# S5 input products from 32-row pieces of split tiles, and the angle sum issued one chunk ahead

## The chip, the cores and the metric

The kernel runs on one core of a Trainium2 chip. The core has a matrix engine (TensorE: PE for its matmuls, PEld for its weight loads), a vector engine (VectorE, DVE), a scalar engine (ScalarE, ACT), a general engine (GpSimd, POOL), and a queue that issues transfers (SyncE, SP). Each engine works through its own queue in the order in which the program puts its instructions there, and an instruction that waits holds back all that stand behind it.

The metric is the device time in microseconds (us); smaller is better. Beside the median of several runs there is one profiled execution, from which all rows of the profile come.

## The reference, cut to what matters

One decoder block works on 256 tokens of 2048 features in float32: a norm, a wide projection `w_in`, two token mixers (S5 and HGRN2), a gated merge, an output projection, and a gated feed-forward network with a short convolution. The change lies in the S5 mixer. Its 1024 input channels `u` form 64 groups of 16, and each group has 64 complex states:

```python
bu_re = einsum('blgc,gpc->blgp', u, b_re)          # input products
bu_im = einsum('blgc,gpc->blgp', u, b_im)
bb_re = coef_re * bu_re - coef_im * bu_im          # hold coefficients
bb_im = coef_re * bu_im + coef_im * bu_re
s     = associative_scan(abar * s_prev + bb)       # along the 256 tokens
y     = einsum(s_re, c_re) - einsum(s_im, c_im) + d * u
```

The kernel folds the coefficients into the input matrices, and turns the complex recurrence into a real one by rotating inputs and states with tables of sines and cosines of the angle per step.

## The kernel before, in words

**The weight stream.** All large products run over tiles of 128x1024 weights. For each tile SP loads `wr`, ScalarE rounds it to `wh` (line 256), VectorE computes the rest `wl = wr - wh`, and TensorE multiplies high and low parts in three products. `wh` and `wl` have three buffers each, so ScalarE and VectorE can be two tiles ahead. `w_in` has 144 such tiles; in the profile one takes TensorE about 2.7 us.

**The side work.** S5 is a generator, `side_s5`, which the loop over the weight tiles resumes after each tile while a meter of estimated VectorE time is not above the one of TensorE (`_dve_cost`, `_pe_cost`; at most two pauses per tile). The tile scheduler then fixes each engine's order. VectorE operations all show line 106, because a helper records them, and so do TensorE's; they are told apart by their tiles.

**One S5 chunk.** There are eight chunks `ct`, each of 128 input channels, that is four pieces `qq` of 32 channels.

- `tables(ct)` makes the rotation tables: GpSimd adds base angles into the tile `w` (line 734, 128x1024), ScalarE rounds it (line 737, which waits for GpSimd), VectorE reduces it, and ScalarE takes sine and cosine (lines 741 to 743).
- `b_place` and `b_trans` write the chunk's input matrix into `zmat`, transpose it on TensorE (`ax<-cf,zmat`), and split matrix and inputs into high and low parts `bc` and `uc` (ScalarE line 260, then VectorE).
- For each piece, 24 GpSimd copies per chunk (line 754, 32x256) then stack three blocks of 32 rows: high, high and low parts of the matrix into `stB`, and high, low and high parts of the inputs into `stU`. Rows 96 to 127 are zero. One matmul over 128 rows so gives the full product of a piece.
- `b_proj(ct, pair)` issues the four matmuls `bu<-u,u` of two pieces into the PSUM tile `bu` (a single buffer of two banks).
- VectorE multiplies `bu` by the tables, combines, runs the scans, and rotates back; `output` multiplies the states by the output matrices (`ax<-u,u`, on 32 columns each).

The products for the next half chunk are issued before the running half is finished, and a chunk's `b_trans` stands in the first half of the chunk before it. `tables(ct+1)` stands in the second half of chunk `ct`, behind the copies for chunk `ct+1` in GpSimd's queue.

Of the kernel before, what the change touches and what calls it, by code (L numbers as in the profile page):

```python
# [17 lines left out]
P = 128  # L18
# [12 lines left out]
# columns of the constant array  # L31
# [5 lines left out]
def _constants():  # L37
# [12 lines left out]
    # within blocks of 32: per level, the columns in second halves of blocks of 2L; then the diagonal  # L50
# [6 lines left out]
# 1/(2 pi) in parts of twelve bits  # L57
# [18 lines left out]
def _dve_cost(name, args, kw):  # L76
    """Estimated microseconds, for the order in which side work is emitted."""
    out = kw.get("out", args[0] if args else None)
    rate = {"tensor_copy": 0.52, "tensor_scalar": 0.52, "reciprocal": 6.3}.get(name, 1.04)
    n = _free(kw["in_"]) if name == "tensor_reduce" else _free(out)  # L80
    return 0.065 + 1.12e-3 * rate * n


def _pe_cost(name, args, kw):
    if name == "transpose":
        return 0.107
    n, m = _free(args[2]), _free(args[1])
    if args[2].dtype == F32R:
        return 0.109 * max(n, 256) / 256 + (0.1 if n < 256 else 0.0)
    if m == 32:  # L90
        return 0.02 + 0.00042 * n
    return 0.213 * max(n, m) / 128


class Metered:
    """An engine that adds up what its instructions are estimated to take."""
# [14 lines left out]
def kernel(  # L111
# [55 lines left out]
    class Chunks:  # L167
        """[128, n, 256] kept in units of four."""
# [102 lines left out]
    def fm_job(wap, c0, nkc, xs, epi, need=None, extra_load=None, wide=False):  # L271
        """psum[n, t] for 256 columns from c0 on; xs(kc) gives the moving pair, or with wide the high part and
        both side by side: the products of the weights' high part then come in two sums to be added up."""
# [30 lines left out]
    def tm_job(wap, c0, width, nkc, kper, xs, epi, need=None, extra_load=None, apart=False):  # L304
        """psum[t, n] for the columns from c0 on; xs(kc) gives the stationary pair."""
# [4 lines left out]
        for g in range(ng):  # L310
            def mm(st, g=g):
# [10 lines left out]
                # all of a row's products together in a last round of several tiles, else the low parts last  # L322
# [22 lines left out]
    def rstd_of(dst, ssum, n, scale, bias=None):  # L345
        """dst = 1/sqrt(ssum*scale + eps) for [128, n]; a Newton step after the square root."""
# [11 lines left out]
    def broadcast_rows(dst, r):  # L358
        """dst[p, j*128 + t] = r[t, j] on every partition."""
# [18 lines left out]
    def warm_up(n, rhs):  # L378
        # matmuls that nothing reads keep the tensor engine's clock up until the first products
# [3 lines left out]
    def table_up():  # L383
        # the square root's table comes in before x does
# [8 lines left out]
    def x_chunk(g, between=None):  # L393
        """Four chunks of x*g, transposed and in two parts; the rows' norms come in after the products."""
# [19 lines left out]
    def behind_x():  # L414
        """What is emitted here is queued behind the last chunk of x."""
# [29 lines left out]
    def normed(ps):  # L445
        """The products of a feature-major job with the rows' norms."""
# [101 lines left out]
    def exp_parts(new, xin):  # L548
        """expm1 of the reduced argument and the power of two, with exp(x) = (1 + e) * s."""
# [20 lines left out]
    def side_s5():  # L570
        # the matrices, long before they are needed
# [6 lines left out]
        # parameters on columns  # L578
# [13 lines left out]
        # lower bound of the forget gate: softmax over two logits, first entry  # L592
# [30 lines left out]
        # angle per step in turns: multiples of 2^-12 and the rest  # L623
# [25 lines left out]
        # coefficients of the zero-order hold  # L649
# [24 lines left out]
        # base angles of the rotation tables  # L674
# [12 lines left out]
        # input matrices with the coefficients in them  # L687
# [14 lines left out]
        # output matrices, transposed  # L702
# [20 lines left out]
        zero = unit()  # L723
        G.memset(zero[96:128, :], 0.0)
        # rows in three blocks of 32: the high and low parts whose products make up one full product
        stB, stU = ([unit(F32R) for _ in range(2)] for _ in range(2))
        for t_ in stB + stU:
            G.tensor_copy(t_[96:128, :], zero[96:128, :])

        def tables(ct):  # L730
            w, r = unit(), unit()
# [4 lines left out]
            yield  # L736
# [16 lines left out]
        def move(dst, src):  # L753
            G.tensor_scalar(out=dst, in0=src.bitcast(F32), scalar1=1.0, scalar2=0.0, op0=ALU.mult, op1=ALU.add)  # L754

        def b_trans(ct):
# [3 lines left out]
            bc, uc = tmp(F32R), tmp(F32R)  # L760
            split_pair(bc[:, 0:T], bc[:, T:2 * T], ax[:, 0:2 * P])
            split_pair(uc[:, 0:T], uc[:, T:2 * T], u_t.at(ct))
            sB, sU = v3(stB[ct % 2], 4), v3(stU[ct % 2], 4)
            for qq in range(4):
                for j in range(3):
                    rows_from, rows_to = slice(32 * qq, 32 * qq + 32), slice(32 * j, 32 * j + 32)
                    hb, hu = (0, 0, 1)[j], (0, 1, 0)[j]
                    move(sB[rows_to, qq, :], bc[rows_from, hb * T:(hb + 1) * T])
                    move(sU[rows_to, qq, :], uc[rows_from, hu * T:(hu + 1) * T])

        def b_proj(ct, pair):
            bu = psb.tile([P, 2, 512], F32, tag="bu", name=f"bu{uid[0]}")
            uid[0] += 1
            sB, sU = v3(stB[ct % 2], 4), v3(stU[ct % 2], 4)
            for a in range(2):
                qq = 2 * pair + a
                for i in range(2):
                    PE.matmul(bu[:, a, i * T:(i + 1) * T], sB[:, qq, i * P:(i + 1) * P], sU[:, qq, :],
                              start=True, stop=True)
            return bu  # L780

        def output(ct, rot):
            """Issues the products of the states of chunk ct and returns what follows them."""
# [23 lines left out]

        tab = yield from tables(0)
# [8 lines left out]
        for ct in range(8):  # L817
            rot = []
            sn, cs = tab
            for pair in range(2):  # L820
# [7 lines left out]
                # the next products, long before they are read  # L828
# [37 lines left out]
    def side_hgrn():  # L866
# [9 lines left out]
        # scores: the diagonal tiles, and in their place first the blocks of 32 on the diagonal; the tiles above  # L876
# [28 lines left out]
        def scores(hg, m):  # L905
            """products of keys with the queries in second halves of blocks of 2m"""
# [65 lines left out]
        # values, per-head norm, gate  # L972
# [247 lines left out]
    def epi_down(b):  # L1220
        def epi(ps):
# [6 lines left out]
            if b == 2:  # L1228
                # what the last block's sum of squares is added to
                V.tensor_reduce(out=prev, in_=ss3[:, :, 0:3], axis=mybir.AxisListType.X, op=ALU.add)  # L1230
                # the square root's table comes in here, and not in the tail
# [58 lines left out]
    def side_run(force=None):  # L1290
        """Emit side work while the vector engine has less to do than the tensor engine, or to the end of the forced one."""
# [99 lines left out]
```

## Time and profile before

| | |
|---|---|
| median of 3 runs | 1447.08 us (1445.60 to 1448.22) |
| span of the profiled execution | 1446.9 us |
| TensorE busy | 1408.5 us (97%) |
| VectorE busy | 1065.1 us (74%) |
| ScalarE busy | 749.1 us (52%) |
| GpSimd busy | 205.6 us (14%) |
| granted TensorE clock, mean | 0.989 |

Busy shares are means over stages with different limits. The S5 chunks lie between about 100 and 440 us, and nearly all of GpSimd's work lies there. TensorE's `w_in` tiles run through the same stretch. Later stages (HGRN2, projections, feed-forward) use GpSimd hardly at all. A row of the grouped view gives an operation's tiles and shapes, its count, its busy time, and the mean of one in ns; a row of the timeline gives the start, the time to the end, and, in brackets, the idle time of the engine ahead of it and what ended that.

### The profile page before, as it was taken

What the parts mean: (1) busy time and instruction counts of PE and PEld (TensorE: products, weight loads), DVE (VectorE), ACT (ScalarE), POOL (GpSimd) and SP (SyncE); (2) the same over time, 40 slices, a digit from 0 to 9 for tenths busy, and PEclk for the clock granted to TensorE, in tenths of its full rate; (3) what the DMA queues carried; (4) which work ended last, traced back from release to release, by engine and by line L of the source; (5) the groups of instructions that cost most, each with busy time, mean ns of one, the idle gap of its engine ahead of it and who ended that gap; (6) DMA issues with size and microseconds to landing.
All of it is one profiled execution on the core that took longest, in us unless ns stands there. A gap on an engine that the chain in (4) does not pass through costs nothing.

```text
span 1446.9 us, 21528 instructions
## 1 busy us (share of the span) xinstructions
PE 1408.5 (97%) x8328; PEld 1209.1 (84%) x8328; DVE 1065.1 (74%) x1435; ACT 749.1 (52%) x944; POOL 205.6 (14%) x230
## 2 busy tenths in 40 slices
PE   9997989899999999999999999999999999999997
PEld 8996887786778988888888888888888888888886
DVE  6978988999996967755677777777777775545454
ACT  5353466565554465445555555555555554434343
POOL 3037416743560100000000000000000000000000
PEclk9999999999999999999999999999999999999999
DMA  7763746565667656766666666666666665666563
GB/s 242 197 210 118 207 154 217 178 181 167 214 184 220 218 175 223 220 213 212 198 188 189 189 189 189 189 189 190 189 189 189 188 188 192 195 198 201 192 194 128
DMA packets 215942, 278.62 MB, mean 193 GB/s; under 512 B 19937, under 2 KB 141041, under 8 KB 215840
## 3 DMA queue, kind: packets, MB, share of 16 engines
q1 hardware_dynamic: 198496, 266.57, 59.6%
q10 hardware_dynamic: 17088, 10.49, 2.3%
q8 instruction: 65, 1.06, 0.3%
q14 instruction: 37, 0.30, 0.1%
q0 software_dynamic: 256, 0.19, 0.0%
HBM read 266.73 MB, written 10.49 MB: 192 GB/s over the span
## 4 chain that ended last, share of the span: by engine, by line
PE 82%; DVE 4%; POOL 3%; issue 1%; ACT 0%; DVEq 0%; ACTq 0%
PE mm L106 74%; PE ax L106 7%; POOL u L754 3%; DVE u L106 3%; DVE wl L106 1%; PE bu L106 0%; ACT wh L256 0%; POOL u L734 0%; ACT u L1262 0%; DVE zmat L106 0%; DVE x2g L106 0%; DVE t L106 0%; ACT t L260 0%; ACT t L1246 0%; DVE fin L106 0%
## 5 line engine op out<-in xcount | busy, mean ns | idle before, releaser
L106 DVE TENSOR_TENSOR wl<-wr,wh 128x1024 fp32r<-128x1024 f32 x480 | 596.4, 1246 | 323.8 <-ACT wh L256 321.6
L256 ACT CAST wh<-wr 128x1024 fp32r<-128x1024 f32 x480 | 502.8, 1051 | 607.3 <-PE mm L106 433.6
L106 PE MATMUL mm<-x2g,wh 128*128 128x512 f32 x1408 | 352.6, 392 | 0.0
L106 PEld LDWEIGHTS mm<-x2g,wh 128*128 128x128 f32 x1408 | 253.3, 189 | 45.3
L106 PE MATMUL mm<-wh,u 128*128 128x512 f32 x1040 | 259.7, 391 | 0.0
L106 PEld LDWEIGHTS mm<-wh,u 128*128 128x128 f32 x1040 | 194.1, 188 | 39.7
L106 PEld LDWEIGHTS mm<-x2g,wl 128*128 128x128 f32 x1408 | 192.0, 190 | 13.6
L106 PE MATMUL mm<-wh,hT 128*128 128x512 f32 x768 | 196.6, 399 | 4.9 <-ACT wh L256 4.9
L106 PE MATMUL mm<-x2g,wl 128*128 128x256 f32 x1408 | 196.4, 282 | 0.0
L754 POOL TENSOR_SCALAR u<-t 32x256 fp32r<-32x256 f32 x192 | 167.5, 874 | 163.1 <-ACT t L260 151.4
L106 PEld LDWEIGHTS mm<-wh,hT 128*128 128x128 f32 x768 | 145.5, 192 | 38.5 <-ACT wh L256 5.4
L106 PE MATMUL mm<-wl,u 128*128 128x512 f32 x520 | 140.6, 390 | 0.0
L106 DVE TENSOR_TENSOR u<-u,u 128x512 f32<-128x512 f32 (+3 forms) x134 | 114.0, 874 | 0.3
L106 PEld LDWEIGHTS mm<-wl,u 128*128 128x128 f32 x520 | 97.4, 188 | 19.9
L106 PE MATMUL mm<-wl,hT 128*128 128x512 f32 x384 | 106.0, 397 | 6.6 <-DVE wl L106 6.6
L106 PE MATMUL mm<-hT,wh 128*128 128x256 f32 x768 | 105.1, 289 | 4.4 <-ACT wh L256 4.4
L106 PEld LDWEIGHTS mm<-hT,wh 128*128 128x128 f32 x768 | 98.5, 196 | 5.6 <-ACT wh L256 4.6
L106 PEld LDWEIGHTS mm<-wl,hT 128*128 128x128 f32 x384 | 72.7, 191 | 24.9 <-DVE wl L106 9.5
L106 DVE SCALAR_TENSOR_TENSOR t<-ub,colC,t 128x256 f32<-128x256 f32 x176 | 73.3, 478 | 0.0
L106 PE MATMUL mm<-hT,wl 128*128 128x256 f32 x384 | 55.1, 286 | 0.0
L106 PEld LDWEIGHTS mm<-hT,wl 128*128 128x128 f32 x384 | 50.3, 195 | 0.2 <-DVE wl L106 0.2
L106 DVE TENSOR_TENSOR_SCAN u<-mag,u 128x256 f32<-128x256 f32 x64 | 47.9, 800 | 0.1
(191 smaller groups left out, 894.3 us busy)
## 6 DMA issues: line engine op xcount, KB each, us to landing
wr<-in_w_up_dram SPq DMA_DIRECT2D x176, 512.0 KB, 4.5
wr<-in_w_in_dram SPq DMA_DIRECT2D x144, 512.0 KB, 4.3
wr<-in_w_down_dram SPq DMA_DIRECT2D x88, 512.0 KB, 4.7
wr<-in_w_out_dram SPq DMA_DIRECT2D x32, 512.0 KB, 4.1
wr<-in_w_proj_s_dram SPq DMA_DIRECT2D x16, 512.0 KB, 4.1
wr<-in_w_proj_hgrn_dram SPq DMA_DIRECT2D x16, 512.0 KB, 4.9
d<-t ACTq DMA_DIRECT2D x28, 256.0 KB, 4.4
rl<-d SPq DMA_DIRECT2D x16, 256.0 KB, 3.8
```

Source lines behind the costliest of these rows:

```text
L106: return fn(*args, **kw)
L256: A.copy(st.wh, st.w)
L754: G.tensor_scalar(out=dst, in0=src.bitcast(F32), scalar1=1.0, scalar2=0.0, op0=ALU.mult, op1=ALU.add)
```

## The change

Three things are edited.

1. The copies of line 754 and the tiles `stB`, `stU` and `zero` go. `b_trans` splits the matrix and the inputs into one tile `c` (`bu_in`). `b_proj` takes 32 rows of it for each piece and adds up three matmuls in PSUM in place of one: high by high, high by low, low by high. The two pieces of a pair alternate, each in its own bank. A pair has 12 matmuls in place of 4.
2. The angle sum moves out of `tables` into `angle_sum`. The sums of chunks 0 and 1 are issued ahead of the first table, and the sum of chunk `ct+1` at the start of chunk `ct`. A pause behind the sum goes.
3. The meter counts a matmul on 32 rows at half the time of one on 128.

The other lines of the diff take comments out.

```diff
@@ _pe_cost
-        return 0.109 * max(n, 256) / 256 + (0.1 if n < 256 else 0.0)
+        return (0.109 * max(n, 256) / 256 + (0.1 if n < 256 else 0.0)) * (0.5 if args[1].shape[0] == 32 else 1.0)
@@ side_s5
-        zero = unit()
-        G.memset(zero[96:128, :], 0.0)
-        stB, stU = ([unit(F32R) for _ in range(2)] for _ in range(2))
-        for t_ in stB + stU:
-            G.tensor_copy(t_[96:128, :], zero[96:128, :])
-        def tables(ct):
-            w, r = unit(), unit()
+        bu_in = {}
+        angles = {}
+        def angle_sum(ct):
+            w = angles[ct] = unit()
             q0 = 4 * ct
             w4 = w.rearrange("p (q i j) -> p q i j", q=4, i=16)
             G.tensor_tensor(out=w4, in0=tabA[:, q0:q0 + 4, :].unsqueeze(3).to_broadcast([P, 4, 16, 16]),
                             in1=tabB[:, q0:q0 + 4, :].unsqueeze(2).to_broadcast([P, 4, 16, 16]), op=ALU.add)
-            yield
+        def tables(ct):
+            w, r = angles.pop(ct), unit()
...
-        def move(dst, src):
-            G.tensor_scalar(out=dst, in0=src.bitcast(F32), scalar1=1.0, scalar2=0.0, op0=ALU.mult, op1=ALU.add)
@@ b_trans
-            bc, uc = tmp(F32R), tmp(F32R)
-            split_pair(bc[:, 0:T], bc[:, T:2 * T], ax[:, 0:2 * P])
-            split_pair(uc[:, 0:T], uc[:, T:2 * T], u_t.at(ct))
-            sB, sU = v3(stB[ct % 2], 4), v3(stU[ct % 2], 4)
-            for qq in range(4):
-                for j in range(3):
-                    rows_from, rows_to = slice(32 * qq, 32 * qq + 32), slice(32 * j, 32 * j + 32)
-                    hb, hu = (0, 0, 1)[j], (0, 1, 0)[j]
-                    move(sB[rows_to, qq, :], bc[rows_from, hb * T:(hb + 1) * T])
-                    move(sU[rows_to, qq, :], uc[rows_from, hu * T:(hu + 1) * T])
+            c = bu_in[ct] = unit(F32R)
+            split_pair(c[:, 0:T], c[:, T:2 * T], ax[:, 0:2 * P])
+            split_pair(c[:, 2 * T:3 * T], c[:, 3 * T:4 * T], u_t.at(ct))
@@ b_proj
-            for a in range(2):
-                qq = 2 * pair + a
-                for i in range(2):
-                    PE.matmul(bu[:, a, i * T:(i + 1) * T], sB[:, qq, i * P:(i + 1) * P], sU[:, qq, :],
-                              start=True, stop=True)
+            c = bu_in[ct]
+            for i in range(2):
+                for j, (hb, hu) in enumerate(((0, 0), (0, 1), (1, 0))):
+                    for a in range(2):
+                        rows32 = slice(64 * pair + 32 * a, 64 * pair + 32 * a + 32)
+                        PE.matmul(bu[:, a, i * T:(i + 1) * T], c[rows32, hb * T + i * P:hb * T + (i + 1) * P],
+                                  c[rows32, (2 + hu) * T:(3 + hu) * T], start=j == 0, stop=j == 2)
@@ side_s5, ahead of the chunks
+        angle_sum(0)
+        yield
+        angle_sum(1)
         tab = yield from tables(0)
...
             sn, cs = tab
+            if 1 <= ct < 7:
+                angle_sum(ct + 1)
```

**GpSimd's order, first chunks.** Before, a piece around the second angle sum (`u_1314` and `u_1733` are the angle tiles of chunks 0 and 1, `t_...` the split parts, `u_1306` to `u_1309` the stacked tiles):

```order
L728 CAST u_1309<-u_1304 32x1024
L734 ISA
L734 TENSOR_TENSOR u_1314<-u_936 128x1024
L754 TENSOR_SCALAR u_1306<-t_1389 32x256
L754 TENSOR_SCALAR u_1308<-t_1390 32x256
...
L754 TENSOR_SCALAR u_1307<-t_1511 32x256
L754 TENSOR_SCALAR u_1309<-t_1512 32x256
L734 TENSOR_TENSOR u_1733<-u_936 128x1024
L754 TENSOR_SCALAR u_1306<-t_1912 32x256 x2
```

Now, all that GpSimd has to do in the S5 chunks:

```order
L731 ISA
L731 TENSOR_TENSOR u_1304<-u_936 128x1024
L731 TENSOR_TENSOR u_1336<-u_936 128x1024
L731 TENSOR_TENSOR u_1781<-u_936 128x1024
L731 TENSOR_TENSOR u_2222<-u_936 128x1024
L731 TENSOR_TENSOR u_2720<-u_936 128x1024
L731 TENSOR_TENSOR u_3070<-u_936 128x1024
```

Before, 48 copies stood between the first two sums; now the sums stand next to each other.

**ScalarE's order, at the second table.** Before:

```order
L256 CAST wh_1670<-wr_1603 128x1024
L256 CAST wh_1699<-wr_1628 128x1024
L737 ACTIVATE u_1734<-u_1733,roundc 128x1024
L256 CAST wh_1717<-wr_1650 128x1024
L256 CAST wh_1739<-wr_1668 128x1024
```

Now:

```order
L256 CAST wh_1610<-wr_1531 128x1024
L736 ACTIVATE u_1681<-u_1336,roundc 128x1024
L256 CAST wh_1647<-wr_1563 128x1024
L256 CAST wh_1665<-wr_1586 128x1024
L740 ACTIVATE u_1681<-u_1336 128x1024
```

The rounding step stands between the splits of the weights as it did; what it waits for now stands early in GpSimd's queue.

**TensorE's order, at one group of input products.** Before:

```order
L106 MATMUL ax_2288<-u_2000,u_1289 32x256 x2
L106 MATMUL mm_2318<-hT,wh_2228 128x256 x16
L106 MATMUL mm_2318<-hT,wl_2229 128x256 x8
L106 MATMUL bu_2343<-u_1308,u_1306 128x256 x4
L106 MATMUL mm_2318<-hT,wh_2260 128x256 x16
```

Now:

```order
L106 MATMUL ax_2213<-u_1931,u_1289 32x256 x2
L106 MATMUL mm_2126<-hT,wh_2153 128x256 x16
L106 MATMUL mm_2126<-hT,wl_2154 128x256 x8
L106 MATMUL bu_2258<-u_1868 128x256 x12
L106 MATMUL mm_2295<-hT,wh_2185 128x256 x16
```

The group stands between weight tiles as before, with 12 matmuls in a row where 4 stood, and reads one tile in place of two.

More of the change, by code (lines that the diff above doesn't have):

```diff
@@ L773, in b_proj @@
             uid[0] += 1
-            sB, sU = v3(stB[ct % 2], 4), v3(stU[ct % 2], 4)
-            for a in range(2):
-                qq = 2 * pair + a
-                for i in range(2):
-                    PE.matmul(bu[:, a, i * T:(i + 1) * T], sB[:, qq, i * P:(i + 1) * P], sU[:, qq, :],
-                              start=True, stop=True)
+            c = bu_in[ct]
[5 more added lines that the diff above has]
+                                  c[rows32, (2 + hu) * T:(3 + hu) * T], start=j == 0, stop=j == 2)
             return bu
```

## The prediction

> **What bounds the kernel now.** I read the slices of the page first, then busy time by stage, then the waits of TensorE in the stage that stands out.
>
> ```profile
> PE   9997989899999999999999999999999999999997
> DVE  6978988999996967755677777777777775545454
> POOL 3037416743560100000000000000000000000000
> 100.00:440.00 340.00, 315.32 (x1658) 261.62 (x1657) 314.97 (x353) 189.32 (x212) 184.71 (x201) 0.96 0.60 183
> 440.00:1380.00 940.00, 939.68 (x5654) 805.63 (x5653) 639.78 (x816) 486.56 (x639) 5.73 (x2) 1.00 0.63 196
> ```
>
> The two last rows are stretches of the span; after the length come the busy times of PE, PEld, DVE, ACT and POOL, the granted clock, the DMA share and GB/s. TensorE is the bound everywhere. From 440 to 1380 us it misses 0.3 us, and nothing is to be had there. In the stretch of the S5 chunks, 100 to 440 us, it stands still for 340 - 315.3 = 24.7 us, and VectorE is almost as full as TensorE (315.0). The change can win only there. The waits of TensorE in this stretch, and one of ScalarE (total us, times, longest):
>
> ```profile
> PE mm L106 <- ACT wh L256: 9.3, 2, 4.9
> PE bu L106 <- POOL u L754: 7.0, 4, 2.5
> PE mm L106 <- DVE wl L106: 6.6, 5, 3.0
> PE bu L106 <- DVE u L106: 1.7, 1, 1.7
> ACT u L737 <- POOL u L734: 23.2, 2, 14.2
> ```
>
> The first four make up the 24.6 us. The largest names ScalarE, but ScalarE itself was held at line 737. The timelines of GpSimd, ScalarE and TensorE at the longer of the two places:
>
> ```profile
> 109.78 26.48 POOL L754 TENSOR_SCALAR u<-t 32x256 fp32r<-32x256 f32 x34
> 136.35 2.17 POOL L734 TENSOR_TENSOR u<-u 128x1024 f32<-128x1024 f32 x1
> 138.55 1.15 ACT L737 ACTIVATE u<-u,roundc 128x1024 f32<-128x1024 f32 x1 [14.24 <-POOL u L734]
> 121.24 1.98 PE L106 MATMUL mm<-wh,hT 128*128 128x512 f32 x8
> 123.05 1.07 PE L106 MATMUL mm<-wl,hT 128*128 128x512 f32 x4
> 140.69 3.65 PE L106 MATMUL mm<-wh,hT 128*128 128x512 f32 x8 [4.92 <-ACT wh L256]
> 144.13 1.16 PE L106 MATMUL mm<-wl,hT 128*128 128x512 f32 x4
> ```
>
> 34 copies run ahead of the angle sum; ScalarE waits 14.2 us for it with the next `wh` behind that instruction; TensorE runs out of weights for 4.9 us. And the stall costs more than itself: the eight matmuls behind it take 144.13 - 140.69 = 3.44 us, where eight of the same kind take 123.05 - 121.24 = 1.81. The granted clock shows the same by stage:
>
> ```profile
> 140.00:200.00 60.00, 54.92 (x323) 48.22 (x324) 52.03 (x58) 32.67 (x39) 22.28 (x26) 0.91 0.55 162
> 200.00:280.00 80.00, 74.19 (x439) 63.33 (x438) 75.84 (x90) 54.69 (x66) 44.44 (x36) 0.98 0.65 205
> 280.00:340.00 60.00, 58.34 (x264) 46.97 (x264) 55.81 (x62) 33.95 (x35) 33.59 (x40) 0.97 0.60 183
> 340.00:440.00 100.00, 95.22 (x447) 75.66 (x448) 95.67 (x103) 52.29 (x56) 48.65 (x51) 0.97 0.64 195
> ```
>
> The lost clock is 60 x 0.09 + 80 x 0.02 + 60 x 0.03 + 100 x 0.03 = 11.8 us. So all that the stalls cost is 24.6 + 11.8 = 36.4 us. By what ended them: GpSimd 9.3 + 7.0 = 16.3 idle, with the clock of the first and third stretch (5.4 + 1.8), 23.5 us; VectorE 6.6 + 1.7 = 8.3, with the second and fourth (1.6 + 3.0), 12.9 us.
>
> **The change, part by part.** *The copies and the early angle sum.* The products wait for no copy, and the sum of a chunk stands a chunk ahead in a queue that is nearly empty, so both kinds of GpSimd wait go: -23.5 us. I see no work that would bring them back: the split parts were made by ScalarE and VectorE before the copies, and the products stand in the same place behind them. Of the moved sum, 2.2 us of GpSimd, nothing else is queued behind.
>
> *VectorE beside GpSimd.* The 192 copies also slow VectorE. The first three rows are from a stretch without GpSimd work (140 to 161 us), the next three from the whole stage (busy us, mean ns):
>
> ```profile
> L106 DVE TENSOR_TENSOR wl<-wr,wh 128x1024 fp32r<-128x1024 f32 x8 | 9.6, 1216 | 1.6 <-ACT wh L256 1.6
> L106 DVE TENSOR_TENSOR u<-u,u 128x512 f32<-128x512 f32 x4 | 2.6, 682 | 0.0
> L106 DVE TENSOR_TENSOR_SCAN u<-mag,u 128x256 f32<-128x256 f32 x4 | 2.4, 670 | 0.0
> L106 DVE TENSOR_TENSOR wl<-wr,wh 128x1024 fp32r<-128x1024 f32 x103 | 134.4, 1318 | 21.4 <-ACT wh L256 20.7 <-ACT u L741 0.6
> L106 DVE TENSOR_TENSOR_SCAN u<-mag,u 128x256 f32<-128x256 f32 x60 | 45.5, 808 | 0.1
> L106 DVE TENSOR_TENSOR u<-u,u 128x512 f32<-128x512 f32 x62 | 45.3, 761 | 0.1
> 288.67 1.93 POOL L734 TENSOR_TENSOR u<-u 128x1024 f32<-128x1024 f32 x1
> 288.84 2.84 DVE L106 TENSOR_TENSOR wl<-wr,wh 128x1024 fp32r<-128x1024 f32 x1 [1.46 <-ACT wh L256]
> ```
>
> The three kinds lose 103 x 0.102 + 60 x 0.138 + 62 x 0.079 = 10.5 + 8.3 + 4.9 = 23.7 us. Not all comes back: the last two rows show a `wl` of 2.84 us that started inside an angle sum, 1.62 longer than an undisturbed one, and the sums stay. Six of them fall between busy VectorE work, so up to 6 x 1.6 = 10 us of loss remain, and VectorE wins 14 to 24 us. Its work in the stage becomes 291 to 301 us.
>
> Is that enough? If all goes as I reckon, the stage shrinks to about 321 us, so VectorE is still 91 to 94% full, close to the 93% (315 of 340) of now. The 12.9 us of stalls that VectorE ended need not all go: bounds 0 and 12.9. I take half, -6.4 us, since VectorE's lag behind TensorE shrinks and its share does not.
>
> *The products.* A group of 4 matmuls over 128 rows becomes one of 12 over 32 rows; there are 8 x 2 = 16 groups. No row has a tile of 32 rows. The nearest ones, a group of transposes, one of `output` and one of the products:
>
> ```profile
> 88.38 1.04 PE L106 MATMUL ax<-cf,u 128*128 128x128 f32 x8
> 89.17 2.16 PE L106 MATMUL mm<-hT,wh 128*128 128x256 f32 x16
> 249.23 1.07 PE L106 MATMUL ax<-u,u 128*32 128x256 f32 x16
> 250.23 2.14 PE L106 MATMUL mm<-wh,hT 128*128 128x512 f32 x8
> 252.21 1.08 PE L106 MATMUL mm<-wl,hT 128*128 128x512 f32 x4
> 253.12 0.64 PE L106 MATMUL bu<-u,u 128*128 128x256 f32 x4
> 253.60 2.00 PE L106 MATMUL mm<-wh,hT 128*128 128x512 f32 x8
> ```
>
> A group now takes 253.60 - 253.12 = 0.48 us, 0.12 a matmul. If the pieces of 32 rows run one after the other, 12 take 1.44. If two pieces run side by side, as the four tiles of 32 columns in `output` seem to (16 matmuls of the same 256 columns in 1.00 us, 0.0625 each), 12 take 0.75. Between them lie the transposes: 0.79/8 = 0.099 each, though they pass only 128 columns, so there the load of 128 columns of weights seems to set the pace; the new matmuls load 128 columns too. I take 0.08, between the tiled row and the weight-bound row: 0.96. Around a tiled group the matmuls behind it start slower: 252.21 - 250.23 = 1.98 against 1.81, 0.17; entering I take at half of that, so 0.25 a group. A group then costs 0.96 + 0.25 - 0.48 = 0.73 us more, with bounds 0.52 and 1.21; 16 groups, +11.7 us (8.3 to 19.4). All of it falls on the engine that is the bound.
>
> Two rules of the Trainium skill weigh on this. TensorE: Matmul & The Clock Gate, LDWEIGHTS, says that a load takes columns/1.2 ns however few rows it has, 107 ns here; if loads queue for one another, an estimate by that page is 12 x 0.107 = 1.28 us a group and +16.8 us in all, and the change, which triples the loads, pays three times for the same weights. TensorEngine Tiling (Array Packing), Key Properties, says that tiles load and multiply in parallel but that a change of mode drains the array; by that the low bound holds. The transposes' 0.099 us speaks for the first, the tiled `output` row for the second.
>
> *The rest.* The five GpSimd instructions ahead of the first chunk (lines 724 and 728) go; nothing waits for GpSimd's first sum but the first table, which was in time. The pause less and the meter's rate move S5's last output from tile 140 to 138 of 144, away from the gated unit that needs it: 0 us. `bu` keeps its single buffer, so its products still wait for VectorE's two multiplications of the half chunk before.
>
> *Sum*: -23.5 - 6.4 + 11.7 = -18.2 us on the span of 1446.9: 1428.7. The median stands 0.2 above the span: **1429 us**.
>
> **The rivals.**
>
> *VectorE takes over the bound.* The six remaining sums hit it while it is full, and its 12.9 us of stalls stay. For it: 95.67 busy of 100 in the last stretch, and its share does not fall. Against: it wins at least 14 us. Then -23.5 + 11.7 to 19.4: 1435 to 1443.
>
> *The stalls only change their name.* TensorE waits at `bu` for VectorE's split of `c` or for the multiplications that free the buffer, as it did once for 1.7 us. This would have to take 18 us, more than one per group, with the order nearly unchanged: 1447, within 3.
>
> *Slower: weights that aren't hidden.* If a piece of 32 rows can't load while the one before it multiplies, each matmul costs its load and its pass:
>
> ```profile
> L106 PEld LDWEIGHTS bu<-u,u 128*128 128x128 f32 x64 | 9.9, 193 | 11.1 <-POOL u L754 10.1
> ```
>
> 0.193 + 0.12 = 0.31 us, 3.8 a group, 3.3 more than now, 16 x 3.3 = 53 us in all, against 30 won: 1470. It decides from a matmul of about (0.48 + 30/16)/12 = 0.2 us on. Against it: the load of 0.193 hides behind 0.12 us steps in every untiled group.
>
> **How the numbers follow.** Forecast 0.66; VectorE as the bound 0.17; renamed stalls 0.07; unhidden loads 0.10. The forecast's own range is 1418 (all 36.4 us go, the products at +8.3, which is 1419, less about the 1.5 us by which the lowest run shown lies under the median) to 1437. The range goes on to the end of the second case: 1418 to 1443; past it lie the last two cases. Differences under 0.2%, 2.9 us, can't be told from none. Faster by more: the forecast and nearly all of the second case, 0.82; the same: the renamed stalls and a little of the second, 0.08; slower: 0.10.
>
> **What would show it.** Right: no ScalarE wait on the angle sum; TensorE's idle time in the stage down from 24.7 to under 10 us and the clock there near 1.00; `wl` at a mean near 1.24 us; a group of 12 products in 0.75 to 1.2 us from its start to the next matmul. VectorE as the bound shows as TensorE's waits on `wl` at 8 us or more with stretches of VectorE at 100%. Wrong altogether: groups of 2.4 us or more, or waits `bu` on VectorE in most groups.

## The result, and the profile after

| | before | after |
|---|---|---|
| median | 1446.86 us (1445.60 to 1448.22, 4 runs) | 1426.43 us (1426.09 to 1427.82, 4 runs) |
| ratio after to before | | 0.9855, 95% interval 0.9841 to 0.9869 |
| span of the profiled execution | 1446.9 us | 1424.0 us |

The change makes the kernel 20 us faster. Forecast were 1429 us, and 1418 to 1443 as the range. The forecast holds. Its reasons hold only in part, and that is what the experiments are about.

The slices of the page after the change (busy tenths in 40 slices of the span):

```profile
PE   9999999999999999999999999999999999999997
POOL 1020000000001000000000000000000000000000
```

The seven and the two eights in TensorE's fourth to eighth slice are gone, and GpSimd is idle but for a few single instructions. The same two stretches as before, with the busy times of PE, PEld, DVE, ACT and POOL, then the clock:

```profile
100.00:440.00 340.00, 339.04 (x1930) 281.56 (x1930) 309.47 (x371) 204.93 (x228) 11.60 (x6) 1.00 0.66 199
440.00:1380.00 940.00, 937.94 (x5633) 804.71 (x5632) 634.13 (x811) 484.09 (x637) 5.77 (x2) 1.00 0.62 195
```

In the stage of the S5 chunks TensorE now stands still for 1.0 us (24.7 before), at a clock of 1.00 (0.96 before). The one wait of TensorE left there:

```profile
PE mm L106 <- DVE wl L106: 0.9, 1, 0.9
```

The groups of the same stage after the change:

```profile
L106 DVE TENSOR_TENSOR wl<-wr,wh 128x1024 fp32r<-128x1024 f32 x113 | 137.7, 1228 | 24.5 <-ACT wh L256 22.7 <-PE ax L106 1.5
L106 DVE TENSOR_TENSOR u<-u,u 128x512 f32<-128x512 f32 x64 | 44.8, 729 | 0.2
L106 DVE TENSOR_TENSOR_SCAN u<-mag,u 128x256 f32<-128x256 f32 x64 | 39.2, 668 | 0.1
```

`wl` went from 1.318 to 1.228 us, a scan from 0.808 to 0.668, the 512-wide products from 0.761 to 0.729. Where the gain stands can be read from two marks. The first is the first matmul of the gated unit, behind `w_in`, in TensorE's timeline, before and after:

```profile
476.87 2.08 PE L106 MATMUL mm<-u,wh 128*128 128x256 f32 x16
```

```profile
452.35 0.28 PE L106 MATMUL mm<-u,wh 128*128 128x256 f32 x1
...
456.79 0.56 PE L106 MATMUL ax<-u,u 128*32 128x16 f32 x44 [0.58 <-issue]
```

The second is the first matmul of the feed-forward network, in the view of one tile (durations in ns, then the first and the last start in us), before and after:

```profile
L106 PE MATMUL mm<-x2g,wh x1408: 387/389/474, 704.5 to 1196.7; 128*128 128x512 f32 x176
```

```profile
L106 PE MATMUL mm<-x2g,wh x1408: 387/390/474, 681.7 to 1173.8; 128*128 128x512 f32 x176
```

At the end of `w_in` the kernel is 476.87 - 452.35 = 24.5 us ahead, at the second mark 704.5 - 681.7 = 22.8, at the end of the span 22.9. So 1.6 us of the lead is given back behind `w_in`. HGRN's small score products (`ax<-u,u`, 16 columns each) run among the gated unit's matmuls in both kernels, but they start 6.9 us behind the first mark before the change and 0.7 us behind it now. Now TensorE stands still there three times, 0.58, 0.55 and 0.62 us, and the trace puts these gaps down to the issue of instructions; before the change it has no such gap there.

### The profile page after: what moved, and what is told of

Same layout as the page of the kernel before. It is cut to its first block, busy times and chain, and to the rows that moved or that the text cites. A ratio compares the mean times of both kernels' runs of the same rounds, so it can differ in the third digit from the quotient of the medians.

```text
span 1424.0 us, 21580 instructions
## 1 busy us (share of the span) xinstructions
PE 1405.9 (99%) x8456; PEld 1206.6 (85%) x8456; DVE 1045.8 (73%) x1435; ACT 751.6 (53%) x946; POOL 32.3 (2%) x33
## 4 chain that ended last, share of the span: by engine, by line
PE 94%; DVE 4%; issue 1%; ACTq 1%; ACT 0%; DMA 0%; POOL 0%; DVEq 0%; POOLq 0%
PE mm L106 85%; PE ax L106 7%; DVE u L106 2%; DVE wl L106 1%; PE bu L106 1%; ACTq L575 0%; DVE t L106 0%; DMA u<-in_s_log_dt_dram 0%; ACTq L577 0%; ACT wh L256 0%; PE dummy L106 0%; ACT u L1258 0%; DVE hT L106 0%; DVE x2g L106 0%; ACT hT L405 0%
## 5 line engine op out<-in xcount | busy, mean ns | idle before, releaser
L106 DVE TENSOR_TENSOR wl<-wr,wh 128x1024 fp32r<-128x1024 f32 x480 | 589.4, 1231 | 317.0 <-ACT wh L256 312.6
L106 PE MATMUL mm<-wh,hT 128*128 128x512 f32 x768 | 193.4, 394 | 0.0
L106 PEld LDWEIGHTS mm<-wh,hT 128*128 128x128 f32 x768 | 142.2, 188 | 33.7 <-issue 2.9
L106 DVE TENSOR_TENSOR u<-u,u 128x512 f32<-128x512 f32 (+4 forms) x142 | 114.0, 826 | 0.5
L106 PE MATMUL mm<-wl,hT 128*128 128x512 f32 x384 | 103.0, 390 | 0.9 <-DVE wl L106 0.9
L1183 ACT ACTIVATE t<-ub,colC 128x256 f32<-128x256 f32 x88 | 47.9, 592 | 0.0
L106 PE MATMUL ax<-wh,u 128*128 128x512 f32 x176 | 43.3, 389 | 0.0
```

The source lines that it names most:

```text
L106: return fn(*args, **kw)
L1183: A.activation(out=av, in_=ub[:, a, 0:T], func=AF.Identity, scale=conv_col(0, n), bias=colC[:, 264 + n:265 + n])
```

## The experiments

Kernels under one line share their runs of the kernel before, whose median is given first. These medians of the kernel before lie between 1448.46 and 1448.88, where its runs beside the change gave 1446.86; so a gain is read within its line. All kernels derived from the change, e1 too, keep the meter's factor of 0.5 unless their line names the meter.

| kernel | median, us | ratio to before (95%) |
|---|---|---|
| *before: 1448.88* | | |
| e1: products and meter, no early sum | 1425.95 | 0.9841 (0.9825 to 0.9858) |
| e2: early sum only, copies kept | 1443.06 | 0.9961 (0.9949 to 0.9973) |
| e3: the change, with the copies running for nobody | 1441.84 | 0.9952 (0.9934 to 0.9970) |
| e5: the change, pieces in turn | 1427.12 | 0.9848 (0.9833 to 0.9862) |
| *before: 1448.46* | | |
| e4: the change, with fills in place of the dead copies | 1430.66 | 0.9885 (0.9861 to 0.9908) |
| e6: the change, low parts on half the columns | 1429.77 | one run |
| e7: the change, meter at the full rate | 1431.06 | 0.9884 (0.9867 to 0.9900) |
| *before: 1448.61* | | |
| e8: products wait for fills | 1460.76 | 1.0086 (1.0072 to 1.0100) |
| e9: the change again | 1425.18 | 0.9842 (0.9829 to 0.9855) |
| e11: meter at the full rate again | 1431.18 | 0.9886 (0.9871 to 0.9900) |
| e10: meter at a quarter | 1425.70 | 0.9839 (0.9825 to 0.9854) |
| *before: 1448.86* | | |
| e12: products wait for fills, in the order of before | 1456.78 | 1.0050 (1.0033 to 1.0066) |

### Each half alone: e1 and e2

e1 is the change with the angle sum left in `tables`, as before:

```diff
         def tables(ct):
+            angle_sum(ct)
             w, r = angles.pop(ct), unit()
+            yield
...
-        angle_sum(0)
-        yield
-        angle_sum(1)
...
-            if 1 <= ct < 7:
-                angle_sum(ct + 1)
```

> The change without its second part: the products come from 32-row pieces, the angle sum is made where it was made before, at the start of each table. Theory (an empty GpSimd queue is enough, the early place of the sum is not needed): ScalarE waits about 2.2 us per table, which its two tiles of lead cover; 1425 to 1430 us, like the whole change (1426.4). Rival (half the gain is the early sum): TensorE waits again for the weights behind the rounding step, 9 to 15 us, so 1436 to 1441 us.

e2 is the kernel before with the early sum and without any edit of copies, products or meter:

```diff
-        def tables(ct):
-            w, r = unit(), unit()
+        angles = {}
+        def angle_sum(ct):
+            w = angles[ct] = unit()
...
-            yield
+        def tables(ct):
+            w, r = angles.pop(ct), unit()
...
+        angle_sum(0)
+        yield
+        angle_sum(1)
...
+            if 1 <= ct < 7:
+                angle_sum(ct + 1)
```

> Before, with the early angle sum alone; all 192 copies stay. Theory (the stalls add up): the two waits behind the angle sum go, 9.3 us idle and about 5 us of clock, and the other stalls stay; 1447 - 14 = 1433 us, within 4. Rival (the copies bound the stage anyway): the time won returns as waits of the products for copies and for VectorE; 1442 to 1447 us.

e1 measured 1425.95: the new products, with the meter's factor, give the whole gain, and the early sum adds nothing to them. e2 measured 1443.06. Its stage in the stretches and its waits of TensorE:

```profile
100.00:440.00 340.00, 318.81 (x1693) 264.97 (x1692) 325.89 (x360) 192.59 (x216) 185.57 (x200) 0.97 0.62 186
```

```profile
PE mm L106 <- DVE wl L106: 8.2, 7, 4.7
PE bu L106 <- POOL u L758: 8.1, 5, 2.6
PE mm L106 <- ACT wh L256: 2.5, 2, 1.8
PE ax L106 <- DVE u L106: 2.5, 1, 2.5
```

ScalarE waits no longer for the sum, and the 9.3 us that TensorE waited behind it are down to 2.5. With the clock lost in that stretch, 5.4 us, the prediction's reckoning makes that 9.3 - 2.5 + 5.4 = 12.2 us. The time fell by 5.8. The waits on VectorE grew from 8.3 to 10.7 us, and those on the copies from 7.0 to 8.1. So a wait that is taken away makes room for others, as long as the copies run.

### What the copies cost without anybody waiting: e3 and e4

e3 lets the 192 copies run in the changed kernel, from `c` into two tiles that nobody reads. e4 puts fills in their place, so that GpSimd is as busy and reads nothing:

```diff
@@ b_trans, e3
+            for qq in range(4):
+                for j in range(3):
+                    rows_from, rows_to = slice(32 * qq, 32 * qq + 32), slice(32 * j, 32 * j + 32)
+                    hb, hu = (0, 0, 1)[j], (0, 1, 0)[j]
+                    for d, h in ((0, hb), (1, 2 + hu)):
+                        G.tensor_scalar(out=v3(dead[d], 4)[rows_to, qq, :], in0=c[rows_from, h * T:(h + 1) * T].bitcast(F32),
+                                        scalar1=1.0, scalar2=0.0, op0=ALU.mult, op1=ALU.add)
@@ b_trans, e4
+            for qq in range(4):
+                for j in range(3):
+                    for d in range(2):
+                        G.memset(dead[d][32 * j:32 * j + 32, :], 0.0)
```

> The whole change, with the 192 GpSimd copies of 32x256 issued again into two tiles that nothing reads. Theory (the copies slow VectorE, and its lateness was what ended 12.9 us of TensorE's stalls): the splits of the weights are back at a mean near 1.32 us, and TensorE's waits for VectorE are back; 1434 to 1440 us. Rival (VectorE was late only as an after-effect of what waited for GpSimd): VectorE's rows are as slow as in the theory, but TensorE keeps its 1.0 idle in the stage; 1426 to 1429 us.

> The change, with 192 GpSimd instructions that fill 32 x 1024 elements of a tile that nobody reads with zeros, at the place where the copies stood: GpSimd is about as busy as with the dead copies, but reads nothing, and nobody waits for it but the next angle sum, a chunk early. Theory by reading (VectorE is slowed because GpSimd reads the same memory beside it): no loss, 1426 to 1430 us, `wl` at a mean of 1.22 to 1.24 us, TensorE's idle time from 100 to 440 us under 3 us. Rival (any busy GpSimd slows VectorE): as with the dead copies, 1437 to 1444 us, `wl` at 1.28 to 1.32 us, 8 us or more of idle time.

e3: the stage, TensorE's waits, and the groups of VectorE and GpSimd:

```profile
100.00:440.00 340.00, 329.07 (x1831) 269.42 (x1830) 321.19 (x358) 193.29 (x216) 171.59 (x200) 0.98 0.62 185
```

```profile
PE mm L106 <- DVE wl L106: 7.4, 8, 2.7
PE bu L106 <- DVE u L106: 2.3, 1, 2.3
PE mm L106 <- ACT wh L256: 0.9, 1, 0.9
```

```profile
L765 POOL TENSOR_SCALAR u<-u 32x256 fp32r<-32x256 f32 x192 | 155.0, 808 | 145.6 <-ACT u L260 123.4 <-DVE u L106 11.2
L106 DVE TENSOR_TENSOR wl<-wr,wh 128x1024 fp32r<-128x1024 f32 x104 | 133.6, 1296 | 13.8 <-ACT wh L256 12.9 <-PE ax L106 0.8
L106 DVE TENSOR_TENSOR_SCAN u<-mag,u 128x256 f32<-128x256 f32 x64 | 47.2, 792 | 0.1
L106 DVE TENSOR_TENSOR u<-bu,u 128x1024 f32<-128x1024 f32 x32 | 38.3, 1213 | 2.3 <-ACT u L743 2.3
```

No engine waits for GpSimd in this stretch any more, and yet 1441.84 - 1425.95 = 15.9 of e1's 22.9 us are lost again. VectorE is slow beside the copies (`wl` 1.296, a scan 0.792), and TensorE waits for it. The product that reads PSUM, `u<-bu,u`, is as fast as ever. The expectation's upper end, 1440, was a little too low.

e4: the stage, and the same groups:

```profile
100.00:440.00 340.00, 336.69 (x1925) 279.70 (x1924) 312.16 (x369) 203.04 (x226) 179.27 (x180) 1.00 0.64 196
```

```profile
L763 POOL MEMSET u<- 32x1024 f32 x172 | 159.0, 949 | 4.6
L106 DVE TENSOR_TENSOR wl<-wr,wh 128x1024 fp32r<-128x1024 f32 x112 | 137.1, 1236 | 22.1 <-ACT wh L256 20.4 <-PE ax L106 1.5
```

Over the whole stage GpSimd is about as busy as in e3, but `wl` stays at 1.236 us and TensorE stands still for 3.3 us. The fills wait for nothing, so they run nearly without a break until 277 us and not at all behind that, while e3's copies come in bursts until 396 us. The stretch that has both, first e3, then e4:

```profile
100.00:280.00 180.00, 172.57 (x1067) 147.21 (x1066) 171.85 (x193) 101.32 (x121) 106.48 (x124) 0.98 0.60 180
```

```profile
100.00:280.00 180.00, 176.69 (x1127) 152.07 (x1126) 168.76 (x204) 109.29 (x128) 175.12 (x178) 1.00 0.62 190
```

There GpSimd is busier in e4 (175.1 us against 106.5), and still TensorE stands still for 3.3 us in place of 7.4, at a clock of 1.00 in place of 0.98; `wl` takes 1.254 us there in place of 1.316 (1.239 in the change). The median of 1430.66 is 0.7 above the range of the theory and 6 below that of the rival; its runs spread from 1428.0 to 1435.9. So it is the copies' reading, and not a busy GpSimd, that makes most of the loss. About 5 us of it comes with any busy GpSimd; where these go the profile, taken of the run of 1428.0, shows in part only.

### The waits without a slow VectorE: e8 and e12

e8 turns e3 around: the kernel before with fills of a dead tile in place of the copies, and two small copies behind each quarter (two more ahead of a chunk's first fills), so that the products wait for GpSimd as before while GpSimd reads next to nothing.

```diff
-                    move(sB[rows_to, qq, :], bc[rows_from, hb * T:(hb + 1) * T])
-                    move(sU[rows_to, qq, :], uc[rows_from, hu * T:(hu + 1) * T])
...
+                for j in range(6):
+                    G.memset(dead[j % 2][32 * (j // 2):32 * (j // 2) + 32, 0:880], 0.0)
+                move(sB[rows_to, qq, 0:8], bc[rows_from, T:T + 8])
+                move(sU[rows_to, qq, 0:8], uc[rows_from, 0:8])
```

> The kernel before, with the 192 copies replaced: for each quarter of a chunk six fills of 32 x 880 elements of a tile that nobody reads, about 0.85 us each, and behind them two copies of 32 x 8 elements into the stacked tiles. The rest of the stacked tiles keeps a constant, so S5's input products are left out in all but form. The products wait for GpSimd, and the angle sum is queued behind it, as before, but GpSimd reads next to nothing beside VectorE. Theory (the copies cost by slowing VectorE, and the waits on them mostly stand in for VectorE's lag): `wl` at 1.22 to 1.25 us, and 1430 to 1437 us. Rival (the waits on GpSimd cost what the prediction read off, 23.5 us, whatever VectorE does): 1442 to 1450 us, with TensorE's waits on `bu` and on ScalarE behind the angle sum at 14 us or more.

It measured 1460.76, beyond either theory, and does not answer the question. The fills depend on nothing, so the scheduler put long runs of them ahead of angle sums and of the small copies, and the longest wait of TensorE became 8.2 us. e12 binds the order: the fills write the stacked tiles themselves, behind the small copies.

```diff
...
+                move(sB[64:96, qq, 0:8], bc[32 * qq:32 * qq + 32, T:T + 8])
+                move(sU[64:96, qq, 0:8], uc[32 * qq:32 * qq + 32, T:T + 8])
+                for j in range(6):
+                    G.memset(sB[0:96, qq, :].bitcast(F32), 0.01)
+                    G.memset(sU[0:96, qq, :].bitcast(F32), 0.01)
```

> As e8, but so that GpSimd's order stays as before: for each chunk eight copies of 32 x 8 elements wait for the split, and behind them 48 fills with a constant of 96 x 256 elements of the stacked tiles themselves, about 0.33 us each, in the order in which the products need them; the fills take the time of the copies and read nothing. S5's input products are left out in all but form. The products wait for GpSimd as before, and so does the angle sum. Theory (waits and a slowed VectorE are both needed for most of the loss): `wl` at 1.21 to 1.25 us, 1431 to 1440 us. Rival (the waits alone cost what they cost before): 1443 to 1452 us.

It measured 1456.78, over the rival's upper end. The longest of TensorE's waits, and the groups:

```profile
PE bu L106 <- POOL u L769: 24.7, 10, 4.9
```

```profile
L106 DVE TENSOR_TENSOR wl<-wr,wh 128x1024 fp32r<-128x1024 f32 x100 | 122.1, 1232 | 36.7 <-ACT wh L256 33.4 <-PE mm L106 3.1
L754 POOL TENSOR_SCALAR u<-t 32x8 fp32r<-32x8 f32 x64 | 62.9, 983 | 171.2 <-DVE t L106 167.0
```

`wl` is as fast as after the change (1.232), and TensorE waits for GpSimd all the same. So waits on GpSimd can cost time beside a VectorE that is not slowed, and the theory that the copies cost only by slowing it finds no support. But e12 asks for more than the kernel before did: eight small copies of 0.98 us stand ahead of the fills, and GpSimd's busy time in the stage leaves (176.57 - 62.9 - 15.7) / 384 = 0.26 us for each fill (15.7 us are its angle sums). So the first products of a chunk wait for 8 x 0.98 + 24 x 0.26 = 14.1 us of GpSimd, where it was 12 x 0.874 = 10.5 before, and 24.7 us of waits stand against 7.0.

What e3 and e12 say: a slow VectorE without the waits gives back 15.9 us of the gain. The waits (longer ones) without a slow `wl` cost more than the whole gain. The 7.0 us that e3 keeps are what is left after the new products, which cost TensorE about 10.1 us (worked out below); so with the waits on GpSimd something like 7.0 + 10.1 = 17 us went in e3. That is an estimate by difference, and the meter's factor is in it. How much the waits of the kernel before would cost beside an undisturbed VectorE stays open.

### The pace of the new products: e5 and e6

In the change the two pieces of a pair, on different rows, take turns. e5 issues the three products of a piece one after the other on the same rows; e6 lets the two products of low parts pass half of the tokens:

```diff
-                for j, (hb, hu) in enumerate(((0, 0), (0, 1), (1, 0))):
-                    for a in range(2):
+                for a in range(2):                                                    # e5
+                    for j, (hb, hu) in enumerate(((0, 0), (0, 1), (1, 0))):
...
+                        n = T if j == 0 else P                                        # e6
+                        PE.matmul(bu[:, a, i * T:i * T + n], c[rows32, hb * T + i * P:hb * T + (i + 1) * P],
+                                  c[rows32, (2 + hu) * T:(2 + hu) * T + n], start=j == 0, stop=j == 2)
```

> The whole change with the twelve products of a group in another order: six on the first 32 rows take turns as three and three with the second, so most neighbours share their rows; all else stands as it did. A group takes 0.90 us now. Theory (two pieces run side by side because neighbours use different rows): two in three neighbours no longer overlap, the group grows towards 12 x 0.12 = 1.44 us, so up to 0.54 x 16 = 8.6 us more, 1431 to 1435 us. Rival A (0.075 us is the pace at which weights load, whatever the rows): group 0.9 us, 1425 to 1428 us. Rival B (a piece's weights can't load while the same rows multiply): 0.31 us a matmul, a group of 3 us or more, 1455 us or more.

> The change, with the two products of low parts in each group passing 128 of the 256 tokens; the corrections by the low parts of the other half of the tokens are left out. A group then has 4 matmuls of 256 columns and 8 of 128. If the load of 128 columns of weights sets the pace of 0.075 us a matmul, the group stays at 0.85 to 0.95 us. If the columns that are passed set it, the group becomes 4 x 0.075 + 8 x 0.0375 = 0.6 us and what the change of mode adds, at most 0.75 us. The whole time says little here: 1420 to 1428 us.

TensorE's timeline around one group, first after the change, then e5, then e6 (where the helper stands at line 108):

```profile
250.84 1.07 PE L106 MATMUL mm<-wl,hT 128*128 128x512 f32 x4
251.75 1.98 PE L106 MATMUL mm<-wh,hT 128*128 128x512 f32 x8
253.56 1.07 PE L106 MATMUL mm<-wl,hT 128*128 128x512 f32 x4
254.56 0.98 PE L106 MATMUL bu<-u 32*128 32x256 f32 x12
255.47 2.12 PE L106 MATMUL mm<-wh,hT 128*128 128x512 f32 x8
257.42 1.08 PE L106 MATMUL mm<-wl,hT 128*128 128x512 f32 x4
```

```profile
254.76 0.98 PE L106 MATMUL bu<-u 32*128 32x256 f32 x12
255.67 2.12 PE L106 MATMUL mm<-wh,hT 128*128 128x512 f32 x8
```

```profile
258.70 0.90 PE L108 MATMUL bu<-u 32*128 32x256 f32 x12
259.53 2.12 PE L108 MATMUL mm<-wh,hT 128*128 128x512 f32 x8
```

A group takes 255.47 - 254.56 = 0.91 us, 0.076 a matmul. The order of the rows makes no difference (0.91), so the pace does not come from neighbours that lie on different rows. With the columns of eight of the twelve halved, the group still takes 0.83 (e6's row shows the first shape for all twelve). Half of 8 x 0.076 = 0.30 us would have gone if the columns set the pace; 0.08 went. That leaves the load of 128 columns of weights, at about 0.07 us, as the likely pace; that it is the load was not measured by itself. Nor does a run show how a matmul of 32 rows passes 256 columns in less than the 0.12 us of one over 128 rows. The whole time of e6, 1429.77, is above its expectation; it is one run, with another order of the side work.

### The meter: e7, e11 and e10

```diff
-        return (0.109 * max(n, 256) / 256 + (0.1 if n < 256 else 0.0)) * (0.5 if args[1].shape[0] == 32 else 1.0)
+        return 0.109 * max(n, 256) / 256 + (0.1 if n < 256 else 0.0)                             # e7, e11
```

> The change, with the planner's meter taking a 32-row matmul at the full rate of 0.109 us, without the factor 0.5; the arithmetic is the same, and side work is emitted a little earlier against the tiles. Theory (the place of the side work does not matter once TensorE waits for nothing): 1425 to 1429 us, within 0.2% of the change. Rival (the factor is part of the gain, because it keeps VectorE's work further apart): above 1430 us.

It came out at 1431.06, as the rival has it, but the change was not run beside it. So the change and this kernel were run again beside each other, with a third at 0.25 in place of 0.5:

> The change itself, on the chip of the two kernels with other meter factors, to compare with them: 1425 to 1429 us.

> The change with the meter at the full rate, without the factor 0.5, once more beside the change on one chip. Theory (the meter's factor is worth a part of the gain, since with the full rate HGRN's small score products come among the last tiles of `w_in`): 3 to 6 us above the change. Rival (the 4 us seen were the other chip): within 2 us of the change.

> The change with the meter's factor at 0.25 in place of 0.5: side work is emitted later still against the tiles. If later is better because less of HGRN's side work meets the tiles of `w_in`: 1420 to 1425 us. If the half rate is already late enough, or S5 ends too late for the gated unit: 1425 to 1432 us.

With the full rate the kernel takes 1431.18, with the half 1425.18, and the intervals of the ratios do not meet: 6.0 us of the gain come from one factor in a table of estimates that changes no arithmetic. A quarter, 1425.70, gives nothing more. With the full rate, then with the half, the start of HGRN's score products in TensorE's timeline:

```profile
435.64 0.77 PE L106 MATMUL ax<-u,u 128*32 128x16 f32 x64
```

```profile
453.42 0.77 PE L106 MATMUL ax<-u,u 128*32 128x16 f32 x64
```

The side work comes 18 us earlier, among the last tiles of `w_in`, and with the full rate TensorE has waits that the change has not:

```profile
PE mm L106 <- ACT t L1046: 1.9, 1, 1.9
PE mm L106 <- ACT wh L256: 1.7, 1, 1.7
PE ax L106 <- DVE u L106: 0.7, 1, 0.7
```

The first stands behind ScalarE, which from 485.93 to 490.63 us loads its tables three times, 1.28 us each (`ACT_TABLE_LOAD`), between the gated unit's sigmoid and a square root of HGRN's norm. But with the half rate TensorE has 2.7 us of gaps in the gated unit that the trace puts down to issue, and with the full rate none. The two profiled executions lie only 2.9 us apart (spans of 1428.2 and 1425.3). Over the whole span TensorE stands still for 20.0 and 19.3 us, and is busy for 1408.2 and 1406.0: so waits make up 0.7 us of the 2.9, and TensorE's longer work 2.2. Why the work takes longer, and where the rest of the 6.0 us lies, is not shown.

## Why the prediction was right, and where it was not

**The bound and the place.** Right. The gain stands at the end of `w_in`, and between 100 and 440 us TensorE's idle time and clock went from 24.7 us and 0.96 to 1.0 us and 1.00.

**First term, -23.5 us for the stalls that GpSimd ended.** They are all gone, but the term was too large and mis-assigned. It gave the late angle sum 14.7 us of them (9.3 idle, 5.4 clock). The early sum, which was to remove these, gained 5.8 us alone (e2) and nothing beside the new products (e1). And with every wait on GpSimd removed but the copies still running, the gain was 7.0 us (e3), where this term and the products would make -23.5 + 11.7 = -11.8; with the products at the 10.1 us of below, the term comes to about 17. The step that failed is the split of the stalls by what ended them: the last releaser of a wait was taken for its only cause, while VectorE was late too. That shows as soon as the waits on GpSimd are out: 7.4 + 2.3 = 9.7 us of waits are ended by VectorE in e3, where it was 8.3 before.

**Second term, -6.4 us for half of the stalls that VectorE ended.** Too small: all but 0.9 us of its 8.3 us of idle time went. VectorE itself won what was reckoned: 113 x 0.090 + 64 x 0.140 + 64 x 0.032 = 10.2 + 9.0 + 2.0 = 21.2 us, within 14 to 24. Its share of the stage did fall, from 315.0 to 309.5 of 340, though the stage now holds 113 `wl` in place of 103. Of the six sums that were to hold it up by 1.6 us each, four fall into the stage; what is seen of them is 64 x 0.047 = 3.0 us in the 512-wide products (0.729 against 0.682 undisturbed) and 113 x 0.012 = 1.4 in `wl`, and one wait of TensorE on `wl`, 0.9 us. What the term left out is the price of the copies beside VectorE: running for nobody they cost 15.9 us (e3), more than the 12.9 that were taken as its upper bound. The first rival, VectorE as the bound, did not come; the second, stalls under a new name, came in e3, at the weights (7.4 us) more than at `bu` (2.3).

**Third term, +11.7 us for the products.** Nearly right. A group takes 0.91 us, and the matmuls beside it start slower: the four ahead take 254.56 - 253.56 = 1.00 in place of 251.75 - 250.84 = 0.91, the eight behind 257.42 - 255.47 = 1.95 in place of 253.56 - 251.75 = 1.81. That is 0.09 + 0.91 + 0.14 = 1.14, against 0.48 and 0.03 before (the next matmuls start at 255.44, so 255.44 - 253.60 = 1.84 behind the group). So 0.63 more a group, and for 16 groups like this one 10.1 us, where 0.73 and 11.7 were forecast. The third rival, weights that aren't hidden, is out by a factor of four (0.076 against 0.31 us a matmul).

The Trainium skill, TensorE: Matmul & The Clock Gate, LDWEIGHTS, has the time of a load go by columns and not by rows. e6 agrees in so far as the moving columns hardly count, but 0.076 us a matmul lies under the page's 0.107 for 128 columns, and the +16.8 us worked out from it did not come.

**The rest, 0 us.** Wrong for the meter. The prediction looked at where the factor moves the last output of S5, and not at HGRN's side work, which follows it and moves too; e11, beside e9, prices the factor at 6.0 us. With the full rate the change gains 1448.61 - 1431.18 = 17.4 us and with the half 23.4, so a quarter of the gain came from an edit that was put at nothing. By which mechanism stays open.

**The sum.** Forecast were -18.2 us on the span, measured -22.9. The other half of the VectorE stalls makes -6.4, the products -1.6, the 1.6 us given back behind `w_in` +1.6: -24.6, which is 1.7 us too much and stays unassigned; the clock term alone, from values rounded to hundredths, is uncertain by 340 x 0.005 = 1.7 us. The meter's 6.0 us have no term of their own in this sum: with the full rate the stalls would not all have gone (3.0 us of waits in the stage against 0.9), and the rest of the 6.0 is not placed. The median lies 2.4 us above the span after the change, where 0.2 was taken; with 2.4 the forecast would have been 1431. The 0.2 set a median beside the span of one execution that need not be the median one: in every run with both on record the time lies 1.7 to 2.2 us above its own span. By the medians the change gains 20.4 us, by the two spans 22.9.

That the forecast came so near is in part luck. The waits on GpSimd were booked some 6 us too high, VectorE's lag and the meter too low, and the errors offset each other.

Of the signs named, all came: no wait of ScalarE on the sum, under 10 us idle, the clock at 1.00, `wl` at 1.228, and the group at 0.91. They did not tell the causes apart, because they follow from the outcome, whichever its cause.

## What to carry to other kernels

The releaser of a wait is the input that came last, not the only late one: before a stall is booked as a gain, ask how late the next input is at that place. Work on GpSimd that nobody waits for can still cost as much as a wait, if it reads memory beside VectorE's operations with two inputs; leaving such copies running costs 15.9 us here, and having TensorE read the pieces itself costs 10.1. Where a table of estimates decides the order, its numbers are part of the change and want a price of their own.

## What was not expected of the hardware

**GpSimd and VectorE hold each other up, whole instructions at a time.** The durations of `wl` (minimum, median and maximum in ns) in the stage, first e3, then the change:

```profile
L106 DVE TENSOR_TENSOR wl<-wr,wh x104: 1192/1218/2954, 102.2 to 438.0; 128x1024 fp32r<-128x1024 f32 x104
```

```profile
L106 DVE TENSOR_TENSOR wl<-wr,wh x113: 1186/1217/2044, 98.9 to 438.4; 128x1024 fp32r<-128x1024 f32 x113
```

The medians are the same, so the mean of 1.296 comes from some operations that are held up for long and not from all being a little slower. GpSimd is held up too. Its timeline in e12, and in the next fence VectorE's at the same time:

```profile
158.59 7.89 POOL L754 TENSOR_SCALAR u<-t 32x8 fp32r<-32x8 f32 x4 [21.73 <-DVE t L106]
166.54 0.56 POOL L768 MEMSET u<- 96x256 f32 x2
167.18 0.19 POOL L754 TENSOR_SCALAR u<-t 32x8 fp32r<-32x8 f32 x1
```

```profile
158.66 1.21 DVE L106 TENSOR_TENSOR u<-u,u 128x1024 f32<-128x1024 f32 x1
...
164.40 1.21 DVE L106 TENSOR_TENSOR wl<-wr,wh 128x1024 fp32r<-128x1024 f32 x1
165.54 2.34 DVE L106 TENSOR_TENSOR u<-bu,u 128x1024 f32<-128x1024 f32 x2
```

A copy of 8 elements a row takes 0.19 us while VectorE runs a product that reads PSUM (`u<-bu,u`). Four of them took 7.89 us over a run of operations with both inputs in SBUF, from 158.66 us until 0.9 us into that product. The Trainium skill, SBUF — State Buffer, Who interferes with whom, says this of the two engines: a VectorE instruction with two SBUF inputs contends with a GpSimd instruction that reads SBUF, not with one that only writes. The runs agree: `wl` 1.296 beside copies and 1.236 beside fills (1.316 and 1.254 in the stretch of both), `u<-bu,u` at 1.213 us in e3. What the fills did hold up were the operations on `zmat`; beside fills, first, and after the change:

```profile
L106 DVE TENSOR_SCALAR zmat<-u,cf x28: 225/546/1045, 103.8 to 348.5; 128x64 f32<-128x64 f32 x28
```

```profile
L106 DVE TENSOR_SCALAR zmat<-u,cf x28: 225/247/254, 102.1 to 344.1; 128x64 f32<-128x64 f32 x28
```

Their median went from 247 to 546 ns, with one input and a write to SBUF on both engines. The same section names copies and `tensor_scalar` among the VectorE operations that can contend with any GpSimd instruction; this agrees, though no run here tells which mode they ran in.
